# Taking key blocks two at a time in the value passes of a prompt attention

## The chip, the cores and the metric

The kernel runs on one core of a Trainium2 chip. The metric is the device time of one launch in microseconds (us). TensorE (PE) multiplies, VectorE (DVE), ScalarE (ACT) and GpSimd (POOL) work on elements, and the SyncE queue (SP) issues transfers. All of them run in order, each on its own list of instructions, and wait for one another by semaphores. TensorE writes into PSUM, a memory of eight banks of 512 fp32 numbers in each of 128 partitions, from which DVE and ACT read.

## What is computed

One inference step of a decoder layer: 1024 prompt tokens and 8 times 4 decode tokens go through an input projection, an attention group with three branches (compressed, selected and window keys), a retention group, an output projection and a convolutional feed-forward net. Of the attention on the prompt, this is what matters here (`g` runs over 2 key groups, `r` over 4 heads in each):

```python
s_s = jnp.einsum('bqgrd,bgqkld->bgrqkl', qg, ks) * scale
p_s = jax.nn.softmax(s_s, axis=-1)
o_sel = jnp.einsum('bgrqkl,bgqkld->bqgrd', p_s, vs)
s_w = jnp.einsum('bqgrd,bwgd->bgrqw', qg, kw) * scale
p_w = jax.nn.softmax(jnp.where(m_w, s_w, NEG), axis=-1)
o_win = jnp.einsum('bgrqw,bwgd->bqgrd', p_w, vw)
out = g[..., 0:1] * o_cmp + g[..., 1:2] * o_sel + g[..., 2:3] * o_win
```

The queries come in 8 blocks of 128. The compressed branch has 63 keys for the whole prompt.

## The kernel before

The kernel is written with a framework that records instructions in the order of the Python program and then, when the program is built, puts each engine's instructions in an order of its own: an instruction recorded earlier has priority, but one recorded later may go ahead where its inputs are ready sooner. So the order in which the Python code emits work is a list of priorities and not the order on the chip.

Prompt attention is the generator `attention` (L1118). Its work is cut into 32 jobs `(i, a, br)`: query block `i` in the order 3, 2, 7, 6, 1, 0, 5, 4, half `a` of the heads, and branch `br` (0: all keys up to the block; 1: the window and the compressed keys). A job has a front and a back.

- **Front** (`front`, L1122): for `br` 0 the step `query` transposes and splits the queries; then two steps `softmax` (L1042), which compute scores on PE into PSUM, the row maximum on DVE (L1072, L1077), the exponential on ACT (L1079), and on POOL the product with the gate over the sum (L1091). The probabilities stand in the tiles `psel`, `vt` (both `PSEL`) or `pwin`.
- **Back** (`values_of`, L1093): for each block of 128 keys, and for `br` 1 for one last block of 64 compressed keys, one step: four transposes on PE (L1103) into one PSUM bank that `t_bank` gives out, one copy of that bank to an SBUF tile `pt` of a ring of four (L1107 on ACT for each third block, L1109 on DVE for the others), then two value products (`mm`, recorded at L466), one for each key group, which add into the bank `OT`. A value product is recorded in the profile as two weight loads and two matmuls on a 128-row, 64-column part of the array (128*64), so a block has four rows; the compressed keys use a 64*64 part. After the last block of `br` 1 the sum is copied to `q_ap(i)` (L1115).

There are 148 blocks. While the back of one job runs, the front of the next is emitted between its steps: `acc` grows by `nf / (FRONT * nblk)` with each back step (L1142), and a front step is emitted when it reaches 1.

What stands beside attention is set by a planner with costs. Every step of `attention` yields a cost (0.85 for a block, 0.43 for `query`, 0.22 for each 128 columns of a softmax step and 0.1 more in `br` 1). `beside` (L1270) emits one step of other work, adds that step's price to `clock[1]`, and then emits steps of attention until their costs, in `clock[0]`, have caught up. The other work is, in this order: what is left of the decode branch (`rest`, 41 steps of 1.32), the load of the output weights (`load_w`, 8 steps of 2.88), and three of the four output projections (`out_project`, 18 steps of 1.63 each), each of which can begin only when both query blocks of its pair are finished. Where attention is behind and nothing else may start, its steps are emitted alone. After the last step comes the last output projection, and then the feed-forward net.

PSUM banks 0 to 5 are given out in a ring by `s_banks` (one bank for a block's transposes, two or four for a softmax step, where a request for two begins at an even bank); bank 6 is `OT`, and bank 7 is used by the output projection and the decode branch.

Of the kernel before, what the change touches and what calls it, by code (L numbers as in the profile page):

```python
# [10 lines left out]
AF = mybir.ActivationFunctionType  # L11
# [48 lines left out]
def hymba(ctx: ExitStack, tc: tile.TileContext, A, O):  # L60
    nc = tc.nc
    V, S, G, T, D = nc.vector, nc.scalar, nc.gpsimd, nc.tensor, nc.sync
# [21 lines left out]
    def pers(n, p=128):  # L84
        o, s = PERS.off[n]
        return pt_[:p, o:o + s]
# [5 lines left out]
    ident = pers("ident")  # L92
# [20 lines left out]
    def q_ap(i):  # L113
        return QBIG[:rows(i), i * 512:(i + 1) * 512]
# [107 lines left out]
    ctr = {"te": 0, "p": 0, "t": 0, "s": 0}  # L222
# [219 lines left out]
    def s_banks(n):  # L442
        if ring:
            return PS[:, 4:6]
        o = -(-ctr["t"] // n) * n % 6
        ctr["t"] = o + n
        return PS[:, o:o + n]

    def t_bank():

        if not ring:
            return s_banks(1)[:, 0]
        ctr["s"] += 1
        return PS[:, ring[ctr["s"] % len(ring)]]
# [10 lines left out]
    def mm(o, a, b, start=False, stop=False):  # L465
        T.matmul(o, a, b, start=start, stop=stop, skip_group_check=True)  # L466
# [469 lines left out]
    o, n = SECT["QC"]  # L936
# [18 lines left out]
    OT = PS[:, 6]  # L955
# [56 lines left out]
    PSEL, PT, PWIN = [], [], []  # L1012

    def job_list(order):
        for i in order:
            for a in range(2):
                for br in range(2):
                    yield i, a, br

    def query(i, a):  # L1020

        tb = t_bank()[:, 0:256]
        for y in range(2):
            o = (2 * a + y) * 128
            T.transpose(tb[:, y * 128:(y + 1) * 128], q_ap(i)[:, o:o + 128], ident)
        for g in range(2):
            src = tb[64 * g:64 * g + 64].rearrange("p (y t) -> p y t", y=2)
            for z in range(2):
                h, l = [QT[a][64 * z:64 * z + 64, o:o + 512].rearrange("p (y g t) -> p y g t", y=2, g=2)[:, :, g] for o in (0, 512)]
                split(h, l, src)  # L1030

    def geometry(i, br):
        if br == 0:
            w0, nw = 0, (i + 1) * 128
            hw = nw if nw <= 512 else nw // 2
        else:
            w0 = max(0, i - 4) * 128
            nw = (i + 1) * 128 - w0
            hw = nw if nw <= 384 else nw // 2
        return w0, nw, hw, nw // hw  # L1040
# [52 lines left out]
    def values_of(i, a, br):  # L1093
        w0, nw, _, _ = geometry(i, br)
        pp = (PSEL, PWIN)[br]
        jobs = [(b * 128, 128, VT[0][:, w0 // 128 + b, br]) for b in range(nw // 128)]
        if br:
            jobs.append((640, 64, VC))
        for z, (c, n, vv) in enumerate(jobs):
            tb = t_bank()[0:n]  # L1100
            for g in range(2):
                for y in range(2):
                    T.transpose(tb[:, (2 * g + y) * 128:(2 * g + y + 1) * 128], pp[2 * y + g][:, c:c + n], ident)  # L1103
            pt = PT[ctr["pt"] % 4]
            ctr["pt"] += 1
            if ctr["pt"] % 3 == 0:
                S.activation(pt[0:n], tb, AF.Copy)  # L1107
            else:
                V.tensor_copy(pt[0:n], tb)  # L1109
            for g in range(2):  # L1110
                mm(OT[64 * g:64 * g + 64, 0:256], vv[:, 64 * g:64 * g + 64], pt[0:n, g * 256:(g + 1) * 256],
                   start=br == 0 and z == 0, stop=n == 64)
            yield 0.85
        if br:
            S.activation(q_ap(i)[:, a * 256:(a + 1) * 256], OT[:, 0:256], AF.Copy)  # L1115
            yield 0.0

    def attention(order, done):  # L1118

        jobs = list(job_list(order))  # L1120

        def front(j):  # L1122
            i, a, br = jobs[j]
            if br == 0:
                query(i, a)
                yield 0.43
            elif a == 0:
                V.tensor_copy(lt["m192"][:, 128:192], lt["cmpm"][:, 56 - 8 * i:120 - 8 * i])
            for y in range(2):
                softmax(i, a, br, y)  # L1130
                yield geometry(i, br)[1] / 128 * 0.22 + 0.1 * br

        yield from front(0)
        for j in range(len(jobs)):
            back = values_of(*jobs[j])
            fr = front(j + 1) if j + 1 < len(jobs) else iter(())
            nf = 3 if j + 1 < len(jobs) and jobs[j + 1][2] == 0 else 2
            nblk = geometry(jobs[j][0], jobs[j][2])[1] // 128 + jobs[j][2]
            alive = [True, True]
            acc = 0.0  # L1140
            while any(alive):
                acc += nf / (FRONT * nblk)  # L1142
                while alive[1] and (acc >= 1.0 or not alive[0]):
                    acc -= 1.0
                    c = next(fr, STOP)
                    alive[1] = c is not STOP
                    if alive[1]:
                        yield c
                if alive[0]:
                    c = next(back, STOP)  # L1150
                    alive[0] = c is not STOP
                    if alive[0]:
                        yield c
            if jobs[j][1:] == (1, 1):
                done.append(jobs[j][0])
# [3 lines left out]
    FRONT = 0.49  # L1159
    ORDER = [3, 2, 7, 6, 1, 0, 5, 4]  # L1160
    finished = []
    main = attention(ORDER, finished)
    main_alive = True
    run(5, ret_gate, building, down, side, SB[1])
# [685 lines left out]
```

## Time and profile before

| | us |
|---|---|
| runs of the kernel | 1548.29, 1543.68, 1547.77 (median 1547.77) |
| profiled execution, its own time | 1553.57 |
| its span, first to last instruction | 1551.8 |
| PE busy in the span | 1488.8 (96%) |
| DVE, ACT, POOL busy | 981.9, 649.8, 617.1 |
| attention on the prompt, first to last row | about 416 to 832 |

The span is what the profile's views divide; the own time of that execution is 1.8 us longer than the span and 5.8 us longer than the median. A busy PE is not a PE at its peak, since matmuls overlap and their ends are modelled: what PE loses is read from the distances between the starts of its rows, and from the granted clock.

### The profile page before, as it was taken

The numbers are of one execution on the slowest core, as the hardware profiler recorded it, in microseconds if no ns is written. First come the engines' busy times: TensorE is split into PE (matmuls) and PEld (weight loads), VectorE is DVE, ScalarE is ACT, GpSimd is POOL, SyncE is SP. The second block draws the span as 40 slices with busy tenths as digits, with TensorE's granted clock in tenths as the row PEclk, the third lists the DMA queues.
The fourth block names the chain that finished last, engine by engine and source line by source line (L and its number), as shares of the span: only waits on it lengthen the run. The fifth ranks groups of instructions, "written<-read, shape, count | busy, mean of one in ns | idle before, by whom it ended". The sixth has DMA issues, their size and how long they took to land.

```text
span 1551.8 us, 28741 instructions
## 1 busy us (share of the span) xinstructions
PE 1488.8 (96%) x10722; PEld 1306.8 (84%) x10722; DVE 981.9 (63%) x1831; ACT 649.8 (42%) x1417; POOL 617.1 (40%) x789
## 2 busy tenths in 40 slices
PE   7999999989999789999999899999999999999998
PEld 5898877757656568787877899999999999999998
DVE  6876525364567664645567888777778777644531
ACT  6464324124445554455445433333333334544430
POOL 3453311350224464545345233333333333544552
PEclk8999999998999899999999899999999999999999
DMA  7452301163431100100002124555554535887662
GB/s 265 145 171 63 96 4 55 31 202 95 149 99 59 55 15 28 31 29 28 28 28 69 65 104 156 163 164 167 172 178 165 170 117 168 274 258 220 206 199 66
DMA packets 129568, 184.54 MB, mean 119 GB/s; under 512 B 20356, under 2 KB 89092, under 8 KB 129428
## 3 DMA queue, kind: packets, MB, share of 16 engines
q1 hardware_dynamic: 127940, 178.08, 36.2%
q0 software_dynamic: 1488, 4.63, 0.9%
q8 instruction: 84, 1.38, 0.4%
q14 instruction: 56, 0.46, 0.1%
HBM read 132.84 MB, written 49.82 MB: 118 GB/s over the span
## 4 chain that ended last, share of the span: by engine, by line
PE 82%; DVE 7%; issue 4%; DMA 2%; POOL 2%; ACT 2%; SPq 1%; DVEq 0%; ACTq 0%; POOLq 0%
PE PS L466 51%; PE PS L235 6%; PE PS L238 5%; PE PS L237 5%; PE PS L1103 3%; PE PS L1241 2%; PE PS L1240 2%; PE PS L1242 2%; POOL pwin L1091 1%; PE PS L779 1%; DVE live L1077 1%; DMA raw<-in_w_in 1%; DVE pt L1109 1%; DMA rbig<-in_xT 1%; PE PS L240 1%
## 5 line engine op out<-in xcount | busy, mean ns | idle before, releaser
L466 PE MATMUL PS<-x,wop 128*128 128x264 f32 x3696 | 457.7, 287 | 7.2 <-ACT wop L122 2.9
L466 PEld LDWEIGHTS PS<-x,wop 128*128 128x128 f32 x3696 | 455.7, 190 | 8.9 <-ACT wop L122 3.1
L466 PE MATMUL PS<-h,wop 128*128 128x264 f32 x1848 | 225.6, 285 | 0.0
L466 PEld LDWEIGHTS PS<-h,wop 128*128 128x128 f32 x1848 | 225.4, 188 | 0.0
L123 POOL TENSOR_TENSOR wop<-sp,wop 128x512 fp32r<-128x512 f32 (+1 forms) x105 | 140.0, 1339 | 182.4 <-ACT wop L122 169.1
L122 ACT ACTIVATE wop<-sp 128x512 fp32r<-128x512 f32 x150 | 90.1, 608 | 205.5 <-PE PS L466 105.4
L123 POOL TENSOR_TENSOR wop<-rawf,wop 128x512 fp32r<-128x512 f32 x42 | 70.9, 1689 | 124.3 <-ACT wop L122 124.2
L1077 DVE TENSOR_REDUCE live<-PS 128x1 f32<-128x640 f32 (+5 forms) x112 | 72.0, 652 | 59.8 <-PE PS L466 47.4
L466 PE MATMUL PS<-kt,qt 128*128 128x320 f32 (+5 forms) x400 | 102.0, 351 | 4.8 <-ACT vt L1079 3.9
L1085 POOL TENSOR_TENSOR live<-live 128x2 f32<-128x2 f32 (+1 forms) x64 | 14.5, 227 | 226.2 <-DVE live L1084 203.8
L235 PE MATMUL PS<-wh,xt 128*128 128x512 f32 (+1 forms) x240 | 94.3, 394 | 10.2 <-ACT xt L122 7.3
L466 PE MATMUL PS<-pt,vt 128*64 128x256 f32 x528 | 80.8, 413 | 6.2 <-DVE pt L1109 4.3
L1109 DVE COPY pt<-PS 128x512 f32<-128x512 f32 (+1 forms) x99 | 66.9, 685 | 30.7 <-PE PS L1103 28.4
L1079 ACT ACTIVATE pwin<-PS,live 128x64 f32<-128x64 f32 (+5 forms) x128 | 61.5, 485 | 58.7 <-DVE live L1077 41.9
L1091 POOL TENSOR_TENSOR pwin<-pwin,live 128x64 f32<-128x64 f32 (+5 forms) x128 | 79.1, 649 | 2.2
L238 PE MATMUL PS<-wh,xt 128*128 128x512 f32 (+1 forms) x192 | 75.3, 393 | 2.8 <-DVE xt L123 2.8
L1240 PE MATMUL PS<-mix,wo 128*128 128x256 f32 (+1 forms) x256 | 75.9, 297 | 1.2 <-ACT mix L122 1.1
L123 DVE TENSOR_TENSOR h<-rawf,h 128x528 fp32r<-128x528 f32 x51 | 44.5, 880 | 51.0 <-ACT h L122 50.7
L235 PE MATMUL PS<-wh,xa 128*128 128x512 f32 (+1 forms) x192 | 75.3, 393 | 1.0 <-ACT qbig L253 0.5
L237 PE MATMUL PS<-wl,xt 128*128 128x512 f32 (+1 forms) x192 | 75.5, 394 | 0.0
L466 PEld LDWEIGHTS PS<-kt,qt 128*128 128x128 f32 x400 | 63.7, 197 | 13.1 <-ACT vt L1079 5.1
L1241 PE MATMUL PS<-mix,wo 128*128 128x256 f32 (+1 forms) x256 | 74.1, 290 | 0.5 <-DVE mix L123 0.5
(388 smaller groups left out, 3082.0 us busy)
## 6 DMA issues: line engine op xcount, KB each, us to landing
rawf<-in_w_ffn_in SPq DMA_DIRECT2D x30, 512.0 KB, 3.3
rawf<-scr_x SPq DMA_DIRECT2D x51, 264.0 KB, 3.5
scr_x<-rbig SPq DMA_DIRECT2D x44, 264.0 KB, 2.6
ws<-in_w_ffn_out SPq DMA_DIRECT2D x64, 176.0 KB, 3.0
scr_s<-ws SPq DMA_DIRECT2D x64, 176.0 KB, 2.2
scr_x<-qbig SPq DMA_DIRECT2D x33, 264.0 KB, 2.1
raw<-in_w_in SPq DMA_DIRECT2D x17, 512.0 KB, 3.6
ga<-in_cache_sel SPq DMA_DIRECT2D x64, 128.0 KB, 2.1
```

Source lines behind the costliest of these rows:

```text
L122: a = S.activation(h, src, AF.Copy)
L123: return a.ins, (eng or V).tensor_tensor(l, src, b32(h), ALU.subtract).ins
L235: T.matmul(ps, xh(i, kk), wh[:, k], start=first, stop=False)
L237: T.matmul(ps, xh(i, kk), wl[:, k], start=False, stop=False)
L238: T.matmul(ps, xl(i, kk), wh[:, k], start=False, stop=end)
L466: T.matmul(o, a, b, start=start, stop=stop, skip_group_check=True)
L1077: V.tensor_reduce(nm, src, AX.XY, ALU.max, negate=True)
L1079: S.activation(d.rearrange("p (b c) -> p b c", b=src.shape[1]), src, AF.Exp, bias=nm, accum_out=st9[:, 12 + e + g:13 + e + g])
L1091: G.tensor_tensor(x, x, f.to_broadcast([128, x.shape[1]]), ALU.mult)
L1109: V.tensor_copy(pt[0:n], tb)
L1240: T.matmul(o, wh, MIX[:, 0, k, 0:n], start=k == 0, stop=False)
L1241: T.matmul(o, wh, MIX[:, 1, k, 0:n], start=False, stop=False)
```

## The change

Blocks are taken in pairs. For each of the two blocks the four transposes and the copy are emitted, and then the value products of both. The first copy of a pair goes to ACT and the second to DVE (the counter is raised before it is tested, and its parity decides over all blocks). The step yields 0.9 per block instead of 0.85, and `acc` grows twice as much for each back step.

```diff
-        for z, (c, n, vv) in enumerate(jobs):
-            tb = t_bank()[0:n]
...
-            pt = PT[ctr["pt"] % 4]
-            ctr["pt"] += 1
-            if ctr["pt"] % 3 == 0:
-                S.activation(pt[0:n], tb, AF.Copy)
-            else:
-                V.tensor_copy(pt[0:n], tb)
-            for g in range(2):
-                mm(OT[64 * g:64 * g + 64, 0:256], vv[:, 64 * g:64 * g + 64], pt[0:n, g * 256:(g + 1) * 256],
-                   start=br == 0 and z == 0, stop=n == 64)
-            yield 0.85
+        for z in range(0, len(jobs), 2):
+            ready = []
+            for c, n, vv in jobs[z:z + 2]:
+                tb = t_bank()[0:n]
...
+                pt = PT[ctr["pt"] % 4]
+                ctr["pt"] += 1
+                if ctr["pt"] % 2:
+                    S.activation(pt[0:n], tb, AF.Copy)
+                else:
+                    V.tensor_copy(pt[0:n], tb)
+                ready.append((n, vv, pt))
+            for e, (n, vv, pt) in enumerate(ready):
+                for g in range(2):
+                    mm(OT[64 * g:64 * g + 64, 0:256], vv[:, 64 * g:64 * g + 64], pt[0:n, g * 256:(g + 1) * 256],
+                       start=br == 0 and z + e == 0, stop=n == 64)
+            yield 0.9 * len(ready)
...
-                acc += nf / (FRONT * nblk)
+                acc += 2 * nf / (FRONT * nblk)
```

## Rows read from the trace of the kernel before

**Rows 1.** The page: busy time of PE, and the granted clock in 40 slices
```profile
PE 1488.8 (96%) x10722; PEld 1306.8 (84%) x10722; DVE 981.9 (63%) x1831; ACT 649.8 (42%) x1417; POOL 617.1 (40%) x789
...
PEclk8999999998999899999999899999999999999999
```

**Rows 2.** Windows: length, busy time of each engine (instructions), clock, DMA share, GB/s
```profile
416.00:832.00 416.00, 386.46 (x2773) 291.74 (x2775) 249.98 (x541) 203.23 (x579) 201.39 (x297) 0.95 0.13 39
832.00:1552.00 720.00, 707.29 (x5752) 704.47 (x5748) 492.77 (x635) 272.20 (x421) 283.46 (x342) 0.99 0.51 166
```

**Rows 3.** Timeline of PE about one group of value passes: start, length, instruction, idle before
```profile
601.13 0.30 PE L1241 MATMUL PS<-mix,wo 128*128 128x288 f32 x1
...
601.27 0.29 PE L1242 MATMUL PS<-mix,wo 128*128 128x288 f32 x1
601.49 0.63 PEld L466 LDWEIGHTS PS<-pt,vt 128*64 128x64 f32 x8 [0.16 <-issue]
601.49 1.08 PE L466 MATMUL PS<-pt,vt 128*64 128x256 f32 x8
602.50 0.19 PEld L1240 LDWEIGHTS PS<-mix,wo 128*128 128x128 f32 x1 [0.39 <-issue]
602.51 0.40 PE L1240 MATMUL PS<-mix,wo 128*128 128x288 f32 x1
...
602.75 0.29 PE L1241 MATMUL PS<-mix,wo 128*128 128x288 f32 x1
```

**Rows 4.** Timeline of PE: the first and the last group of value passes, of 99
```profile
423.75 1.12 PE L466 MATMUL PS<-pt,vt 128*64 128x256 f32 x4
...
832.33 0.65 PE L466 MATMUL PS<-pt,vc 64*64 64x256 f32 x4
```

**Rows 5.** The tile pt: who waited for it (us, times)
```profile
  PEld PS L466: 13.6, 22
  PE PS L466: 7.4, 12
```

**Rows 6.** The transposes, L1103: who waited for them (us, times)
```profile
  ACT pt L1107: 42.0, 24
  DVE pt L1109: 28.4, 38
```

**Rows 7.** Groups by line: the copies, busy and mean ns, idle before
```profile
L1109 DVE COPY pt<-PS 128x512 f32<-128x512 f32 (+1 forms) x99 | 66.9, 685 | 30.7 <-PE PS L1103 28.4 <-PE PS L466 1.6
L1107 ACT ACTIVATE pt<-PS 128x512 f32<-128x512 f32 (+1 forms) x49 | 28.9, 595 | 43.2 <-PE PS L1103 42.0 <-PE PS L466 1.0
```

**Rows 8.** Waits of PE from 416 to 832 us: total, times, longest
```profile
PE PS L466 <- ACT vt L1079: 3.9, 4, 1.3
PE PS L1103 <- ACT pwin L1079: 3.3, 3, 1.5
```

**Rows 9.** Windows, columns as in rows 2
```profile
560.00:720.00 160.00, 154.03 (x1153) 125.19 (x1151) 89.71 (x194) 78.26 (x240) 75.53 (x136) 1.00 0.09 25
802.00:832.00 30.00, 26.43 (x178) 18.50 (x179) 18.83 (x38) 12.87 (x33) 11.88 (x17) 0.94 0.04 12
720.00:730.00 10.00, 9.54 (x63) 7.64 (x62) 5.38 (x13) 5.21 (x15) 7.40 (x8) 0.89 0.18 53
```

**Rows 10.** Timeline where attention is alone: two blocks whose copies PE waits for
```profile
802.44 0.60 ACT L1107 ACTIVATE pt<-PS 128x512 f32<-128x512 f32 x1 [1.86 <-PE PS L1103]
...
803.09 0.65 PE L466 MATMUL PS<-pt,vt 128*64 128x256 f32 x4 [0.69 <-ACT pt L1107]
...
805.02 0.36 PE L466 MATMUL PS<-ma 128*128 128x192 f32 x1 [0.69 <-ACT pt L1107]
```

**Rows 11.** Timeline of PE: the first and the last of eight transposes in a row
```profile
605.37 0.27 PE L1103 MATMUL PS<-pers,vt 128*128 128x128 f32 x1
...
606.13 0.27 PE L1103 MATMUL PS<-pers,psel 128*128 128x128 f32 x1
```

More of the change, by code (lines that the diff above doesn't have):

```diff
@@ L1098, in values_of @@
             jobs.append((640, 64, VC))
-        for z, (c, n, vv) in enumerate(jobs):
-            tb = t_bank()[0:n]
-            for g in range(2):
-                for y in range(2):
-                    T.transpose(tb[:, (2 * g + y) * 128:(2 * g + y + 1) * 128], pp[2 * y + g][:, c:c + n], ident)
-            pt = PT[ctr["pt"] % 4]
-            ctr["pt"] += 1
-            if ctr["pt"] % 3 == 0:
-                S.activation(pt[0:n], tb, AF.Copy)
-            else:
-                V.tensor_copy(pt[0:n], tb)
-            for g in range(2):
-                mm(OT[64 * g:64 * g + 64, 0:256], vv[:, 64 * g:64 * g + 64], pt[0:n, g * 256:(g + 1) * 256],
-                   start=br == 0 and z == 0, stop=n == 64)
-            yield 0.85
+        for z in range(0, len(jobs), 2):
[3 more added lines that the diff above has]
+                for g in range(2):
+                    for y in range(2):
+                        T.transpose(tb[:, (2 * g + y) * 128:(2 * g + y + 1) * 128], pp[2 * y + g][:, c:c + n], ident)
+                pt = PT[ctr["pt"] % 4]
[6 more added lines that the diff above has]
+            for e, (n, vv, pt) in enumerate(ready):
+                for g in range(2):
+                    mm(OT[64 * g:64 * g + 64, 0:256], vv[:, 64 * g:64 * g + 64], pt[0:n, g * 256:(g + 1) * 256],
+                       start=br == 0 and z + e == 0, stop=n == 64)
+            yield 0.9 * len(ready)
         if br:
```

## The prediction

> **What bounds the kernel now.** I read the page first: PE is busy for 96% of the span, the next engine for 63%, and the granted clock is low only in short pieces [rows 1]. So time comes from PE or not at all. The windows then divide the span [rows 2]. After 832 us PE is busy for 707.3 of 720 us, and the change touches nothing there. Attention lies between 416 and 832 us, with PE busy for 386.5 of 416 us. Within it the stretch from 560 to 720 us is full, 154 of 160 us at clock 1.00 [rows 9], because an output projection fills every hole. There a wait costs nothing, and only what PE itself does or loses counts.
>
> What PE loses there is in the timeline [rows 3]. Matmuls of 288 columns start 0.13 us apart (601.13, 601.27). The value passes work on a 128*64 part of the array, everything about them on 128*128. From the start of the last matmul before a group of them (601.27) to the second one behind it (602.75) it takes 1.48 us. Eight rows of value passes take 8 x 0.1075 = 0.86 us; 0.1075 is the step by which the merged rows grow, (1.08 - 0.65) / 4, from eight rows to four (the row of four is of the 64*64 part, [rows 3, 4]). Two distances of 0.13 make 0.26. What is left, 0.36 us, is the price of changing to the small part and back: the weight loads stand still for 0.16 us before and 0.39 us behind the group, waiting for nothing that the profile names [rows 3]. I take **0.36 us for each group**, however long it is. Counted by weight loads, the 148 blocks lie in 99 such groups [rows 4]: 64 of one block, 27 of two, 8 longer. The builder already joins blocks, in 49 of 147 places. All groups cost 99 x 0.36 = 36 us.
>
> **The change part by part.**
>
> *Groups.* 148 blocks become 80 pair steps, 68 of them with two blocks (branches of odd length leave one over). Were every pair kept whole and joined with its neighbour as often as blocks are now (a third of the places), there would be 148 - 68 - 26 = 54 groups, 45 fewer: -16.2 us. Were nothing joined more than now: 0. More groups than now would be a loss, up to 148, which is +18 us; since the change emits the passes of a pair next to each other, I leave that end at +1.8 us, five groups. Within a pair the passes are neighbours in priority but not ready together: the second block's transposes end 0.44 us later (four at 0.11 us [rows 11]) and its copy takes 0.685 us instead of 0.595 [rows 7], so the builder sees a hole of up to half a microsecond and may put other work into it. I take 7 pairs in 10 kept whole and one joint in five between steps: 148 - 48 - 16 = 84 groups, 15 fewer, **-5.4 us**. That is nearer to the end where little changes, because the trace shows joints in a third of the places only.
>
> *Waits for the copies.* PE waited for `pt` 12 times, 7.4 us in all [rows 5]. Where attention is alone this is a whole copy: PE transposes, waits 0.69 us for ACT, and goes on [rows 10]. In a pair the two copies run beside each other on two engines, and one wait serves two blocks. Bounds: -7.4 us, and on the other side the rival below; I take somewhat less than half, **-3 us**.
>
> *Copies moved.* ACT gets 74 instead of 49, DVE 74 instead of 99. That is 25 x 0.685 = 17.1 us off DVE and 25 x 0.595 = 14.9 us onto ACT [rows 7], which are busy for 250 and 203 of 416 us in this stage [rows 2]. Neither is the bound, and PE covers both; if the cover were gone, it would be the difference, -2.2 us. The queue behind matters more: ACT stood 42.0 us waiting for transposes, with exponentials behind that wait; DVE 28.4 us, with row maxima behind it [rows 6]. ACT's part grows by half and DVE's falls by a quarter. Who waits for these in the end is PE, for ACT's exponentials, 7.2 us in the two largest entries [rows 8]. If those waits grew by a half: +3.6 us; if earlier maxima took half away: -3.6 us. I take 0, between ends of equal size.
>
> *Front steps.* With `acc` growing twice as fast for half as many steps, a job's softmax steps come at most one block earlier (eight blocks: before the first and third instead of the second and fourth). That is priority alone; it lies within the same 3.6 us, and I take 0. The number of PSUM banks requested is the same. No transfer is moved, and none is issued in the part that changes, so SP's list is untouched; POOL's products keep their number and order.
>
> *The planner.* 148 x 0.05 = 7.4 more units of cost for the same work. The other work pays 41 x 1.32 + 8 x 2.88 + 54 x 1.63 = 165.2 units, unchanged; attention costs 192.7 units by the code before and 200.1 after. What is emitted alone thus grows from 27.5 to 34.9 units, about five blocks with their share of softmax (200.1 / 148 = 1.35 units each). Price: from 802 to 832 us the last 18 blocks are alone; PE is idle for 3.6 of 30 us, and the clock of 0.94 takes 1.8 us more [rows 9]. That is 5.4 / 18 = 0.3 us a block, and five make **+1.5 us** (0 if the builder covers them, +3 if they stall twice as much).
>
> *A rule on the clock.* PE did eight transposes in a row, 605.37 to 606.13 us, at 0.11 us each, in a stretch with clock 1.00 [rows 9, 11]. Longer runs of transposes thus cost nothing here, and the term is 0. The Trainium skill, "TensorE: Matmul & The Clock Gate", Part 4, says against this change that PE transposes do not count as busy in the way matmuls do, so that the full clock does not set in for them; by that, runs twice as long would cost. The trace does not bear it out while matmuls stand about the runs; it is the fourth rival.
>
> *Sum.* -5.4 - 3 + 0 + 1.5 = -6.9 us. On the profiled execution's own 1553.6 us that is 1546.7; it lay 5.8 us above the median, so I set the same difference against the median of 1547.8: **1540.9 us**, given as 1541. About 0.3% (4.6 us) is what a measurement of this kernel can tell from no change.
>
> **The rivals.**
>
> 1. *Pairs stay whole nearly everywhere.* That the passes of a pair are emitted side by side speaks for it; the hole between their copies speaks against it. 54 to 65 groups, -16.2 to -12.2 us, with -5 of waits and +1.5: 1528 to 1532 us. Chance 0.15.
> 2. *It doesn't do what it says.* The builder splits pairs as freely as it joined blocks, the count of groups stays between 92 and 99, and the waits pass to the second copy: -2.5 at most, with +1.5 of the planner, 1546.8 to 1549.3 us. For it: a third of the joints exist already, and the stretch that is full has no waits to give back. Chance 0.21.
> 3. *Slower: PE waits for the second copy of a pair.* Place: stretches with little other work, while the decode branch runs up to 550 us (about 22 pairs) and where attention is alone (about 14). After eight transposes nothing fills PE until the second copy ends; each such wait costs the 0.69 us of [rows 10]. The 3 us of waits are then not had either, and of the sum 5.4 - 1.5 = 3.9 us of gain remain: six such waits beyond today's eat them, and 20 make 13.8 - 3.9 = +9.9: 1558 us. Against it: front steps come earlier and can fill. Chance 0.18.
> 4. *The clock falls more often* behind longer runs of transposes. One fall costs 1.1 us of PE's work (0.89 over 10 us [rows 9]); one more in each of 32 jobs would be +35 us, less the 6.9: 1576 us. Against it: [rows 11]. Chance 0.03.
>
> **How the numbers follow.** My forecast, 1536 to 1546 us, has 0.43; the rivals have 0.15, 0.21, 0.18 and 0.03. Faster by over 0.3% means under 1543.1: four fifths of the forecast's case and all of the first rival, 0.34 + 0.15, and a little of the second: 0.51. Slower means over 1552.4: the third and fourth and a tail of the second, 0.23. Between them 0.26. The range reaches from 1529, near the first rival's lower end, to 1556 in the third; beyond lie the upper half of that rival (0.09), the fourth (0.03) and tails of the first and of the forecast, some 2 in 10.
>
> **What would show it.** In the trace of the changed kernel the groups of value passes should number about 84, with eight rows the commonest length; the stretch with an output projection beside should still be full at clock 1.00, but hold more blocks. PE's waits for `pt` should fall from 7.4 us to about 4. ACT should show 74 copies, and its waits for transposes should grow. More blocks should stand between the end of the third output projection and the last value pass. I am wrong if the groups fall and the stage is no shorter, or if the stage is shorter with as many groups as now; and if the time goes up, rows of PE waiting for `pt` must show it, or the third rival is wrong as well.

## The result: slower by 0.8%, and the profile after

| | before | after |
|---|---|---|
| median of the runs, us | 1547.8 (1543.7 to 1550.5) | 1559.6 (1555.0 to 1561.2) |
| ratio | | 1.0079 [1.0060, 1.0098] |
| span of the profiled execution, us | 1551.8 | 1556.2 |
| its mean granted clock | 0.976 | 0.981 |
| span times clock, us | 1514.6 | 1526.6 |
| groups of value passes | 99 | 105 |

The kernel became slower, by 11.8 us between the medians. The two profiled executions lie only 4.4 us apart, because that of before lay 5.8 us above its median and held more time at the lower of the clock's two levels, half of full speed (75 us against 58). The last row but one takes the clock out, roughly: it is how long the span would be if all of it had run at the upper level. By that row the execution of after is 12 us longer, but these two lie at opposite ends. Over the runs the same product has a median of 1518 us before (the five sets of 21 to 33 runs beside the experiments, 1517.8 to 1518.2) and of 1523.4 after (five runs, 1521.9 to 1526.6), at clocks of 0.981 and 0.979. So roughly half of the loss is left when the clock is taken out, and the other half goes with a lower clock. A pair of single executions can mislead by as much: up to the first group of value passes, which starts 0.4 us apart in the two, the low clock would account for a difference of 4.5 us.

The page after (busy time of PE, and the clock in 40 slices) answers to [rows 1]:

```profile
PE 1492.0 (96%) x10722; PEld 1307.8 (84%) x10722; DVE 969.3 (62%) x1806; ACT 663.4 (43%) x1442; POOL 618.6 (40%) x789
...
PEclk9999999999999899999999899999999999999999
```

The windows of attention and of what follows answer to [rows 2], with the same columns; then the decode part of the stage by itself (416 to 548) and the stretch behind the third output projection (784 to 832):

```profile
416.00:832.00 416.00, 387.97 (x2774) 291.49 (x2776) 236.12 (x514) 214.15 (x598) 200.22 (x295) 0.97 0.13 39
832.00:1556.00 724.00, 708.85 (x5748) 705.44 (x5744) 493.52 (x635) 272.73 (x421) 281.38 (x342) 0.99 0.51 165
416.00:548.00 132.00, 116.14 (x788) 74.97 (x789) 87.52 (x205) 71.31 (x201) 62.57 (x82) 0.92 0.21 66
784.00:832.00 48.00, 42.97 (x299) 30.81 (x299) 27.35 (x55) 24.63 (x64) 24.00 (x33) 0.96 0.09 27
```

Attention takes the 416 us that it took, now at a clock of 0.97 where it had 0.95: what the clock gave back (5 us) the order of the work lost. Behind it the rest is 4 us longer.

**The pairs were split.** The timeline of PE, where an output projection fills the holes, shows one split pair (start, length, instruction):

```profile
602.22 0.29 PE L1245 MATMUL PS<-mix,wo 128*128 128x288 f32 x1
602.44 0.65 PE L466 MATMUL PS<-pt,vt 128*64 128x256 f32 x4
603.02 0.40 PE L1246 MATMUL PS<-mix,wo 128*128 128x288 f32 x1
603.26 0.29 PE L1244 MATMUL PS<-mix,wo 128*128 128x288 f32 x1
603.48 0.65 PE L466 MATMUL PS<-pt,vt 128*64 128x256 f32 x4
604.07 0.40 PE L1245 MATMUL PS<-mix,wo 128*128 128x288 f32 x1
604.31 0.30 PE L1246 MATMUL PS<-mix,wo 128*128 128x288 f32 x1
```

Two groups of four rows stand 1.04 us apart, and the builder has put two matmuls of the projection into the hole between them. Counted by weight loads there are 105 groups, 73 of one block, 25 of two and 7 longer, where [rows 4] were the ends of 99. Of the 68 pairs 35 stand whole. The rows show the price of a group once more: from the last matmul before the first group (602.22) to the second one behind it (603.26) it takes 1.04 us; without four rows of 0.1075 us and two distances of 0.13 us, 0.35 us are left.

**The waits for the copies fell in this kernel.** The first fence is the tile `pt` (its copies, then who waited for it), the second the transposes, now L1105, and who waited for them; they answer to [rows 5, 7] and [rows 6]:

```profile
L1111 DVE COPY pt<-PS x74: 662/690/694, 419.2 to 830.6; 128x512 f32<-128x512 f32 x64, 64x512 f32<-64x512 f32 x10
L1109 ACT ACTIVATE pt<-PS x74: 576/597/608, 421.6 to 830.3; 128x512 f32<-128x512 f32 x68, 64x512 f32<-64x512 f32 x6
...
  PEld PS L466: 8.7, 19
...
  PE PS L466: 3.1, 8
```

```profile
  ACT pt L1109: 52.0, 32
  DVE pt L1111: 30.7, 32
```

The pairs alone do not do it. In the changed kernel with the old cost of 0.85 (pair_cost85, below) PE waits for `pt` as long as before, 7.5 us:

```profile
  PE PS L466: 7.5, 14
```

**What PE waits for instead** stands in its waits from 416 to 832 us (total, times, longest), to be held against [rows 8]:

```profile
PE PS L1105 <- ACT pwin L1079: 3.9, 4, 2.8
PE PS L466 <- ACT qt L122: 3.2, 5, 1.0
PE PS L1105 <- ACT vt L1079: 2.8, 4, 1.0
PE PS L763 <- DVE pdp L753: 2.6, 2, 1.7
PE PS L1105 <- ACT psel L1079: 2.3, 3, 1.5
PE PS L1105 <- POOL pwin L1091: 1.7, 1, 1.7
PE PS L466 <- ACT pt L1109: 1.7, 4, 0.8
```

Summed over all its entries from 406 to 834 us, PE's listed waits are 29.7 us before and 30.1 after. Those for copies went from 8.3 to 4.6, those for exponentials and gate products from 13.4 to 14.5, those for the split queries `qt` from 0.6 to 3.9. In pair_cost85 the same three are 8.2, 9.7 and 3.5 us. That kernel has the pairs, the copies and the earlier front steps as well, and of the three shifts it shows only that of `qt`. So in these traces the fall for the copies and the rise for the exponentials came with the cost.

### The profile page after: what moved, and what is told of

Same layout as the page of the kernel before. It is cut to its first block, busy times and chain, and to the rows that moved or that the text cites. A ratio compares the mean times of both kernels' runs of the same rounds, so it can differ in the third digit from the quotient of the medians.

```text
span 1556.2 us, 28756 instructions
## 1 busy us (share of the span) xinstructions
PE 1492.0 (96%) x10722; PEld 1307.8 (84%) x10722; DVE 969.3 (62%) x1806; ACT 663.4 (43%) x1442; POOL 618.6 (40%) x789
## 4 chain that ended last, share of the span: by engine, by line
PE 82%; DVE 9%; issue 3%; DMA 2%; ACT 2%; POOL 1%; SPq 0%; DVEq 0%; ACTq 0%; POOLq 0%
PE PS L466 49%; PE PS L235 6%; PE PS L238 5%; PE PS L237 5%; PE PS L1105 4%; PE PS L1245 2%; PE PS L1244 2%; PE PS L1246 2%; PE PS L779 1%; DMA qbig<-in_w_ffn_in 1%; DVE live L1077 1%; PE PS L685 1%; POOL pwin L1091 1%; DMA pers<-in_const 1%; PE PS L240 0%
## 5 line engine op out<-in xcount | busy, mean ns | idle before, releaser
L122 ACT ACTIVATE wop<-sp 128x512 fp32r<-128x512 f32 x150 | 90.3, 608 | 203.4 <-PE PS L466 99.3
L1085 POOL TENSOR_TENSOR live<-live 128x2 f32<-128x2 f32 (+1 forms) x64 | 14.5, 226 | 242.6 <-DVE live L1084 218.7
L235 PE MATMUL PS<-wh,xa 128*128 128x512 f32 (+1 forms) x192 | 75.0, 392 | 0.7 <-DVE hn L246 0.6
L237 PE MATMUL PS<-wl,xa 128*128 128x512 f32 (+1 forms) x192 | 73.7, 384 | 0.0
L238 PE MATMUL PS<-wh,xa 128*128 128x512 f32 (+1 forms) x192 | 73.5, 383 | 0.0
```

The source lines that it names most:

```text
L122: a = S.activation(h, src, AF.Copy)
L235: T.matmul(ps, xh(i, kk), wh[:, k], start=first, stop=False)
L237: T.matmul(ps, xh(i, kk), wl[:, k], start=False, stop=False)
L238: T.matmul(ps, xl(i, kk), wh[:, k], start=False, stop=end)
```

## Experiments

Each ratio is to the kernel before, run between the others on the same chip. "Decode part" means attention up to the first output projection, in which the decode branch stands beside it and 40 blocks pass (38 to 44 in six of the others). The last column is the median over the runs of span times clock, with 1518 for the kernel before.

| kernel | cost per block | median us | ratio [95%] | groups | span times clock |
|---|---|---|---|---|---|
| after | 0.90 | 1559.6 | 1.0079 [1.0060, 1.0098] | 105 | 1523.4 |
| copies_only | 0.85 | 1552.3 | 1.0028 [1.0010, 1.0046] | 108 | 1520.4 |
| cost_only | 0.90 | 1579.7 | 1.0189 [1.0169, 1.0210] | 107 | 1529.4 |
| cost80 | 0.80 | 1545.7 | 0.9980 [0.9963, 0.9997] | 101 | 1516.7 |
| pair_cost80 | 0.80 | 1556.8 | 1.0061 [1.0038, 1.0085] | 104 | 1514.7 |
| pair_cost85 | 0.85 | 1549.2 | 1.0012 [0.9995, 1.0030] | 103 | 1516.5 |
| pair_bare | 0.85 | 1551.1 | 1.0011 [0.9995, 1.0026] | 103 | 1518.4 |
| pair_cost95 | 0.95 | 1544.8 | 0.9977 [0.9958, 0.9995] | 107 | 1516.4 |
| pair_rev | 0.85 | 1543.9 | 0.9969 [0.9953, 0.9985] | 90 | 1513.4 |
| rev90 | 0.90 | 1551.5 | 1.0020 [1.0003, 1.0038] | 89 | 1520.5 |
| rev95 | 0.95 | 1543.0 | 0.9954 [0.9938, 0.9970] | 90 | 1510.6 |
| after_wo | 0.90 | 1557.6 | 1.0049 [1.0030, 1.0068] | 105 | 1522.7 |
| after_own | 0.90 | 1558.6 | 1.0065 [1.0044, 1.0085] | 101 | 1521.8 |
| after_early | 0.90 | 1557.8 | 1.0067 [1.0043, 1.0091] | 105 | 1522.6 |
| before_early | 0.85 | 1545.3 | 0.9976 [0.9957, 0.9994] | 105 | 1515.0 |
| rev95_early | 0.95 | 1572.5 | 1.0137 [1.0098, 1.0176] | 88 | 1518.2 |
| after_d85 | 0.85, from block 41 on 0.90 | 1552.9 | 1.0038 [1.0018, 1.0058] | 108 | 1516.7 |
| after_o85 | 0.90, from block 41 on 0.85 | 1558.8 | 1.0066 [1.0042, 1.0089] | 107 | 1518.6 |

### The change taken apart

One part of the change at a time in the kernel before:

```diff
 copies_only
-            if ctr["pt"] % 3 == 0:
+            if ctr["pt"] % 2:
 cost_only
-            yield 0.85
+            yield 0.9
```

> The kernel before, with only the copies alternating between ACT and DVE (74 and 74 instead of 49 and 99). Theory A: 1552 to 1558 us, with longer waits of PE for exponentials. Theories P and S: 1545 to 1549 us, DVE's relief being worth 2 us at most.

> The kernel before, with only the cost of a block raised from 0.85 to 0.9. Theory P (planner: attention is emitted more slowly beside the other work, so more of it is left alone and PE has holes there): 1552 to 1556 us, and the stretch between the end of the third output projection and the first row of the last one grows from 42.8 to about 50 us. Theory A (copies on ACT hold up the exponentials) and theory S (the pair steps themselves: passes held back, softmax steps moved): 1546 to 1550 us.

The copies cost 0.3% (0.1 to 0.5); 1552.3 us is the lower edge of theory A's window. The cost alone, one constant, makes the kernel 1.9% slower, far beyond every window that I had set, though the stretch without a projection before the last one did grow to 51.3 us, as theory P had it. Then the whole change without its cost, and once more with the copies divided as before:

```diff
 pair_cost85 (and pair_bare)
-            yield 0.9 * len(ready)
+            yield 0.85 * len(ready)
 pair_bare
-                if ctr["pt"] % 2:
+                if ctr["pt"] % 3 == 0:
```

> The changed kernel with the cost of a block put back from 0.9 to 0.85; pairs and alternating copies stay. Theory P: 1549 to 1553 us, the last stretch alone back to about 43 us. Theories A and S: 1556 to 1561 us.

> The changed kernel with the cost at 0.85 and each third copy on ACT as before: only the order in pairs and the doubled growth of acc remain. Theory S: 1555 to 1560 us. Theories P and A: 1545 to 1550 us, and no more groups of value passes than 100.

Both are the kernel before, within the measurement (pair_bare misses its window by 1 us and has 103 groups where at most 100 were expected). So the pairs, with the copies either way, bring nothing and cost nothing, and the loss comes with the 0.9.

### The cost at other values

The constant set to 0.8 in the kernel before, and to 0.8 and 0.95 in the changed one:

```diff
 cost80
-            yield 0.85
+            yield 0.8
 pair_cost80, pair_cost95
-            yield 0.9 * len(ready)
+            yield 0.8 * len(ready)
...
+            yield 0.95 * len(ready)
```

> The kernel before with the cost of a block lowered from 0.85 to 0.8. Theory P (each block of attention that is moved from beside other work to a stretch alone costs about 1 us, so the time follows the number of blocks alone): fewer alone, 1541 to 1547 us. Theory T (0.85 is a tuned point; any other cost shifts the whole order of priorities and loses): 1553 us or more.

> The changed kernel with the cost at 0.8. Theory P: below the 1549 us of the cost 0.85, 1541 to 1547 us. Theory T: 1553 us or more.

> The changed kernel with the cost at 0.95. Theory P: more blocks alone than at 0.9, 1564 to 1575 us. Theory T: anything above 1550 us, not necessarily above the 1559 us of the cost 0.9.

The answer is ragged. With pairs, 0.80, 0.85, 0.90 and 0.95 take 1556.8, 1549.2, 1559.6 and 1544.8 us. Two theories fall at once. "The value of before is the best one" falls, because 0.95 with pairs and 0.80 without them are faster, both only just clear of the noise. "A higher cost leaves more blocks alone at the end" falls as the cause: between the third and the last output projection stand 22 blocks before, 26 after, and 28 with 0.95, which is the fastest of the three. With the clock taken out the four are 1514.7, 1516.5, 1523.4 and 1516.4 us. By this measure what 0.80 loses goes with its clock (0.976 in the median of the runs), and only 0.90 stands out.

### Pairs that hold

The builder splits a pair because the first block is ready before the second. Emitting the passes of the second block first takes that reason away, since whoever waits for the second copy has the first already:

```diff
 pair_rev
-            for e, (n, vv, pt) in enumerate(ready):
+            for e, (n, vv, pt) in enumerate(reversed(ready)):
...
-                       start=br == 0 and z + e == 0, stop=n == 64)
-            yield 0.9 * len(ready)
+                       start=br == 0 and z + e == 0, stop=br == 1 and z + 2 >= len(jobs) and e == len(ready) - 1)
+            yield 0.85 * len(ready)
 rev90, rev95: the same with 0.9 and 0.95
```

> The changed kernel with the cost at 0.85 and the value passes of a pair in reverse order: the block whose copy is ready last goes first, so that nothing can come between the two. If a group of value passes costs 0.36 us and its splitting by the builder was why pairs gained nothing: at most 85 groups instead of 103, and 1541 to 1545 us. If groups are not what counts: fewer groups and 1548 to 1552 us.

> The changed kernel at its own cost of 0.9, with the value passes of a pair in reverse order. If fewer groups are worth about 5 us whatever the planner's cost: 90 groups or fewer, 1552 to 1556 us. If the gain at 0.85 was a lucky arrangement: 1557 us or more.

> The same at a cost of 0.95, where the pairs in plain order took 1544.8 us. If fewer groups are worth about 5 us whatever the cost: 1538 to 1542 us. If the gain at 0.85 was a lucky arrangement: 1544 us or more.

A pair that holds is one row of eight in the timeline of pair_rev:

```profile
608.21 0.49 PE L1105 MATMUL PS<-pers,pwin 128*128 128x128 f32 x3
608.63 1.08 PE L466 MATMUL PS<-pt,vt 128*64 128x256 f32 x8
609.64 0.33 PE L1105 MATMUL PS<-pers,pwin 128*128 128x128 f32 x1
```

There are 42 groups of one block and 43 of two, 90 in all. At each cost the reversed kernel is the faster one: by 0.43, 0.59 and 0.23 per cent at 0.85, 0.90 and 0.95 (differences of the ratios, each give or take 0.25, so that the third is not clear of noise), which is 6.7, 9.1 and 3.6 us for 13, 16 and 17 groups fewer. That is 0.42 us a group on average, and 0.26 with the clock taken out, on either side of the 0.36 of the prediction, though the single values run from 0.2 to 0.6 and the reversal moves other work too. So the price was about right and the count was wrong. The windows were not all met: 90 groups stand where at most 85 were expected, rev90 lies 0.5 us below its window, and rev95 between its two. **rev95 is faster than both kernels**, 0.9954 [0.9938, 0.9970].

### Where 0.9 loses: the handover examined

The kernel after once more, for a second profile:

> The changed kernel once more, for a second look at its trace. If its losses are the schedule's and not one execution's, the first output projection starts at 548 to 550 us again, some 28 us behind the last value passes of the decode branch, and the stretch from the 500th feed-forward product to the end takes 620 us again; if they are chance, 539 to 543 us and 617 us.

Its landmarks agree with the first to 1 us (first output projection at 548.0 against 548.7 us), so the order makes the difference, not the execution. Against pair_cost85 the traces differ in two places. The first output projection starts at 548.7 us against 539.1, of which 8.8 us arise between the last value passes of the decode branch and that start (27.9 against 19.1 us). And in the feed-forward part the second half of the first products takes 230.6 us against 226.9. In the handover the splits of the output weights on ACT (`wo`, L122) stand behind the branch's last products (L784), and those wait for the last transpose of its new keys (L821). Three kernels pulled at this chain, and two carried the last edit elsewhere:

```diff
 after_wo: priority for the splits of the output weights
-            split(WO[q][:, 0, k], WO[q][:, 1, k], st, (V, G)[z % 2])
+            with tc.high_priority(offset=MP):
+                split(WO[q][:, 0, k], WO[q][:, 1, k], st, (V, G)[z % 2])
 after_own: the transpose L821 into a bank outside of the ring
-            tb = t_bank()[:, 0:64]
+            tb = XB[:, 448:512]
 after_early, before_early, rev95_early: L820 to L824 moved ahead of the branch's scores
```

> The changed kernel (cost 0.9), with the splits of the output weights raised in priority by 300, so that they stand ahead of the softmax steps in ACT's and DVE's order. Theory W (at 0.9 ACT reaches these splits 7 us late, behind three softmax steps, and the first output projection starts late by as much): the projection starts within 20 us of the last value passes of the decode branch, and the time falls to 1549 to 1553 us. Rival (the late splits only mark a stage that is slow for other reasons): the splits move, and 1557 to 1561 us remain.

> The changed kernel (cost 0.9); the decode branch's transpose at L821 writes to a corner of bank 7 instead of the next bank of the ring that it shares with prompt attention. Theory B (at 0.9 that transpose draws a bank that a softmax step still holds, so the decode branch ends 6 us late, and with it the load of the output weights and the first output projection): the branch's last passes (L784) stand right behind its other value passes, the projection starts within 22 us of these instead of 27, and the time is 1551 to 1555 us. Rival (any shift of the order changes the time by as much, and this place is one of many): 1556 to 1562 us although L784 moves up.

> The changed kernel (cost 0.9), with the transpose of L821 and its two copies emitted at the start of the selected branch, some steps before they are needed, still with a bank of the ring. Theory B: as with a bank of its own, 1551 to 1555 us. Rival: 1556 to 1562 us.

> The kernel before (blocks one by one, cost 0.85) with the same move of L821; there too the passes of L784 come 5 us behind the other value passes of the decode branch. Theory B: 1542 to 1546 us. Rival: 1547 to 1555 us.

> Pairs in reverse order at the cost 0.95 (1543.0 us), with the same move of L821. There the decode branch's last passes are already in place, so theory B gives no gain, 1541 to 1545 us; the rival anything from 1540 to 1555 us.

None of the three brought the time back. In after_wo the splits did not start earlier, since they wait for L784, so theory W was not put to the test. In after_own and after_early the transpose came at 508 and 498 us instead of 524, yet L784 started at 526.2 and 522.6 against 527.2, behind value passes of the branch (L779) that now ended later, at 526 and 522 us. Behind these L784 follows at once, as theory B asked. after_early began its output projections 4.5 us earlier than the kernel after, after_own 1.6 us, and their runs are no faster for it. So that one transpose, its bank and the gap before L784 are not the cause. The same edit made the kernel before 0.24% faster, as theory B had it, and rev95 1.8% slower, beyond both windows: such an edit moves the time by as much as the whole change did.

The last two kernels divide the cost by place:

```diff
 after_d85
-            yield 0.9 * len(ready)
+            yield (0.85 if ctr["pt"] <= 40 else 0.9) * len(ready)
 after_o85
-            yield 0.9 * len(ready)
+            yield (0.9 if ctr["pt"] <= 40 else 0.85) * len(ready)
```

> The changed kernel with a cost of 0.85 for the first 40 blocks, about those that stand beside the decode branch, and of 0.9 from there on. Theory H (0.9 loses at the handover from the decode branch to the output projections): the handover is as with 0.85 throughout, the first output projection starts near 539 us instead of 548, and the time is 1549 to 1551 us. Rival L (0.9 loses later, among the output projections and behind them): 1556 to 1560 us, and the feed-forward part is 3 us longer than before. Rival S (the order is scattered by any such edit, and no place owns the loss): a time that is neither, below 1547 or above 1561, or one of the two with the landmarks of the other.

> The other way round: 0.9 for the first 40 blocks and 0.85 from there on. Theory H: the late handover stays (first output projection near 548 us), 1556 to 1560 us. Rival L: 1549 to 1551 us, with the feed-forward part as short as before. Rival S: this one and its mirror image don't add up: both near one of the two times, or one outside of 1547 to 1561 us.

**By the time, more of the loss goes with the decode part.** With 0.85 there, 0.41% of the 0.79 come back (give or take 0.28); with 0.9 there and 0.85 behind it nearly all of the loss stays. after_d85 lies 2 us above the window that theory H had set. But with the clock taken out the place is not shown: after_d85 has 1516.7 us and after_o85 1518.6, against 1523.4 with 0.9 throughout and 1516.5 with 0.85 throughout. By that measure 0.85 in either half brings most of the loss back, and what after_o85 still loses in time goes with its clock (0.977 against 0.981 before). The feed-forward part is short in both (227.7 and 227.4 us). It does not follow the cost either: it is as short in after_wo and after_early (227.3 and 227.5 us), which have 0.9 throughout, and long in rev95 (229.6 us), the fastest kernel.

The timelines show the handover. In the kernel after (PE, then ACT):

```profile
519.47 1.92 PE L779 MATMUL PS<-ga,ptd 128*32 128x128 f32 x16
...
523.88 0.27 PE L821 MATMUL PS<-pers,qbig 64*128 64x64 f32 x1
...
527.18 0.41 PE L784 MATMUL PS<-vcd,ptd 128*32 128x128 f32 x4
...
548.72 0.59 PE L1244 MATMUL PS<-mix,wo 128*128 128x288 f32 x1
...
527.67 3.90 ACT L122 ACTIVATE wo<-stg 128x1024 fp32r<-128x1024 f32 x4 [0.81 <-PE PS L784]
```

In after_d85:

```profile
517.52 0.27 PE L821 MATMUL PS<-pers,qbig 64*128 64x64 f32 x1 [0.91 <-ACT pwin L1079]
...
522.08 1.39 PE L779 MATMUL PS<-ga,ptd 128*32 128x128 f32 x21
523.21 0.27 PE L784 MATMUL PS<-vcd,ptd 128*32 128x128 f32 x1
...
542.49 0.59 PE L1244 MATMUL PS<-mix,wo 128*128 128x288 f32 x1
...
523.84 3.90 ACT L122 ACTIVATE wo<-stg 128x1024 fp32r<-128x1024 f32 x4 [1.05 <-PE PS L784]
```

In the kernel after the transpose L821 comes behind the last value passes (L779), and L784 5.8 us behind those (527.18 against 521.39); in after_d85 it comes ahead of them, and L784 follows at once. Yet this gap does not decide the time. The kernel before, at 0.85, has it too, and starts its output projections still later:

```profile
523.80 1.26 PE L779 MATMUL PS<-ga,ptd 128*32 128x128 f32 x16
...
525.88 0.27 PE L821 MATMUL PS<-pers,qbig 64*128 64x64 f32 x1
...
529.33 0.41 PE L784 MATMUL PS<-vcd,ptd 128*32 128x128 f32 x4
...
554.73 0.29 PE L1240 MATMUL PS<-mix,wo 128*128 128x288 f32 x1
```

after_own, as slow as the kernel after, does not have it:

```profile
525.34 1.12 PE L779 MATMUL PS<-ga,ptd 128*32 128x128 f32 x16
526.29 0.39 PE L784 MATMUL PS<-vcd,ptd 128*32 128x128 f32 x4
...
547.08 0.38 PE L1244 MATMUL PS<-mix,wo 128*128 128x288 f32 x1
```

PE also waits longer for exponentials and gate products in the decode part. These are its waits for them from 406 to 545 us in the kernel after, 10.3 us with the entries not shown:

```profile
PE PS L1105 <- ACT pwin L1079: 3.5, 3, 2.8
...
PE PS L1105 <- ACT psel L1079: 2.3, 3, 1.5
PE PS L1105 <- POOL pwin L1091: 1.7, 1, 1.7
PE PS L1105 <- POOL psel L1091: 1.2, 1, 1.2
```

and in after_d85, 5.1 us in all:

```profile
PE PS L835 <- ACT pwin L1079: 1.0, 1, 1.0
PE PS L821 <- ACT pwin L1079: 0.9, 1, 0.9
...
PE PS L1105 <- POOL psel L1091: 0.9, 1, 0.9
PE PS L1105 <- ACT vt L1079: 0.7, 1, 0.7
```

The same sum is 6.3 us in the kernel before, 5.2 in pair_cost85, 8.9 in after_o85, 12.1 in cost_only and 13.2 in after_early. But it is 8.0 in pair_bare and 8.8 in rev95, the fastest of all, so it does not decide it either. Where in the order the kernel with 0.9 loses, which priority causes it, and why 0.95 escapes (its first output projection starts at 535.4 us), was not found out.

**Where cost_only and rev95_early lose.** The larger part of their loss goes with the clock. The windows from 420 to 570 us, of rev95, rev95_early and cost_only in this order:

```profile
420.00:570.00 150.00, 140.44 (x990) 96.03 (x986) 97.68 (x227) 86.16 (x232) 73.46 (x93) 0.95 0.21 65
```

```profile
420.00:570.00 150.00, 134.13 (x769) 83.69 (x769) 81.58 (x194) 70.52 (x198) 58.96 (x78) 0.76 0.20 61
```

```profile
420.00:570.00 150.00, 132.42 (x780) 82.18 (x777) 92.44 (x204) 67.30 (x188) 60.24 (x77) 0.82 0.20 61
```

The clock was granted at 0.76 and 0.82 there, against 0.95 in rev95, and PE did 769 and 780 instructions where rev95 did 990. Why it fell was not examined. Taken over the spans, rev95_early loses 58.3 us to the clock (1576.3 x 0.037) and rev95 29.3 (1540.8 x 0.019): 29 of the 35.5 us between them. cost_only loses 50.4, 13 more than the profiled execution of before, of the 22 us between them. The profiled execution of after loses 29.6, less than that of before; over the runs it is the other way round, as said with the result.

## Why the prediction was wrong

The forecast was 1541 us and the range ended at 1556; the time is 1559.6. Two terms of the sum failed, the groups and the planner: they make 7.6 and 8.9 of the 18.7 us between the -6.9 us of the forecast and the +11.8 measured.

- **The step "Groups" failed.** It had 7 pairs in 10 kept whole and 84 groups. They became 105, beyond the five more that I had left as its other end, and at 0.36 us each that is +2.2 us instead of -5.4. Only 35 of the 68 pairs stand whole instead of 48, and steps are joined in 8 places instead of 16; before, 30 of these same pairs of neighbours already stood together. I had seen the reason, the hole between the two copies, and given it too little weight. The price itself was about right, 0.35 us by the rows of the kernel after. Pairs that hold, in reversed order, are whole in 50 cases.
- **The step "Waits for the copies" hit its number by luck**: PE's waits for `pt` on its own row fell from 7.4 to 3.1 us, where about 4 was forecast. The mechanism, one wait that serves two blocks, did not do it, because pair_cost85 has the same pairs and 7.5 us. For "Copies moved" and "Front steps" I took 0. In the kernel after, PE's waits for exponentials and split queries rose by 4.4 us, more than the bound of 3.6, and the sum of PE's waits stayed; but in pair_cost85, with the same copies and front steps, these waits are 13.2 us, where the kernel before has 14.0. So the 0 was about right for these two steps taken together, and the rise came with the cost.
- **The step "The planner" was mis-sized, and it decided.** I priced 7.4 units of cost as five blocks alone at the end, +1.5 us and 3 at most. Seven more blocks did stand alone (44 against 37, in the three gaps between output projections), but the change from 0.85 to 0.90 costs the paired kernel 10.4 us, or 6.9 with the clock taken out. I had read the cost as an amount, and it is a place in an order; where in that order the time is lost stays open. The 192.7 units of the working come out as 194.0 from the costs of the code, which leaves the 7.4 as it is.
- **The rivals.** The second (the builder splits as freely as before, 92 to 99 groups, 1546.8 to 1549.3 us) is nearly what the pairs do by themselves: 103 groups, 1549.2 us. The third, with the fourth one of the two for a slower kernel, had the sign right for a wrong reason. It asked for rows of PE waiting for `pt`, and those fell. The first did not happen unless forced, and then it is worth less than the 12 to 16 us that I gave it, because 90 groups remain.
- **The fourth rival**, the clock behind longer runs of transposes, was hardly put to the test, because the builder split these runs too: those of eight transposes and more, counted by weight loads, went from 19 to 26. The time at the low clock is 75 us in the profiled execution of before and 58 in that of after, but over the runs the clock is 0.981 and 0.979, a difference within what it varies by from run to run (0.977 to 0.981 for the kernel after). The Trainium skill, "TensorE: Matmul & The Clock Gate", Part 4, which says that transposes do not hold the clock up, would by itself have had the time at the low clock rise. No clear cost of that kind shows in this case, and no run here tests it on runs twice as long throughout.

## What to carry to other kernels

Where a builder sorts instructions by readiness, emitting work side by side does not keep it side by side: take away the reason to split (here, by emitting the part that is ready last first), and count the groups in the trace. A constant of a planner is not an amount that can be priced by the units it adds; try several values, and compare an edit with its rival at each of them, since here the same edit is 0.8% slower at 0.90 and 0.2% faster at 0.95. A wait that is removed is a gain only if the sum of the engine's waits falls. And compare the clock over several runs before one execution is blamed or cleared.

## What was not expected of the hardware and the order

- A group of value passes on the small part of the array carries a price of its own, 0.35 us by the rows of the kernel after: 13 to 17 fewer went with 3.6 to 9.1 us.
- Nineteen kernels with the same arithmetic lie between 1543 and 1580 us. Much of the upper part of that spread goes with the granted clock in the decode part, 0.76 to 0.95 in the windows above; with the clock taken out they lie between 1511 and 1529 us.
- Two executions can show the clock the wrong way round: 0.976 before and 0.981 after in the profiled ones, 0.981 and 0.979 in the medians of the runs. Span times clock varies less between executions of the kernel before than the span does (a spread, as standard deviation, of about 1.7 us against 3), so it is the better comparison, over several runs.
